# A two-layer encoder trunk: squares, latents and a table warm-up at the start, and another order of steps around the gated units of each half

## The chip, the cores and the metric

The kernel runs on one core of one Trainium2 chip. The metric is the device time of one execution in microseconds (us), as the median of several runs. A core has TensorE (PE; its weight loads are PEld), VectorE (DVE), ScalarE (ACT), GpSimd (POOL) and SyncE (SP), which here issues the loads of weights. All data is float32. A matrix product is made of three matmuls: every operand is split into a high half that the fast float32 format ("fp32r") holds, and a low half, the rest; high·high, high·low and low·high are added up in PSUM.

## The reference

One sequence of 512 tokens, 1024 channels, two layers. Layer 0 mixes with a short gated convolution and an 8-head latent attention side by side; layer 1 is a Conformer convolution module. Each has a squared-ReLU MLP of width 4096 behind it. Every part stands between two RMS norms.

```
def conformer_conv(h, w_pw1, b_pw1, w_dw, b_dw, ln_g, ln_b, w_pw2, b_pw2):
    u = h @ w_pw1 + b_pw1
    a, g = jnp.split(u, 2, axis=-1)
    u = a * jax.nn.sigmoid(g)                 # the gated units
    u = depthwise_conv(u, w_dw) + b_dw        # 31 taps over time
    u = jax.nn.silu(layer_norm(u, ln_g, ln_b))
    return u @ w_pw2 + b_pw2
...
for i in range(2):
    h = rms_norm(x, g[0])
    m = parallel_conv_mla(h, ...) if i == 0 else conformer_conv(h, ...)
    x = x + rms_norm(m, g[1])
    h = rms_norm(x, g[2])
    x = x + rms_norm(squared_relu_mlp(h, mlp_w1[i], mlp_w2[i]), g[3])
```

In layer 0, h goes through a combined projection: five blocks of 128 columns are the latents of queries (three) and of keys and values (two), each with an RMS norm of its own; a sixth is the rotary key; twelve more feed the gated convolution.

## The kernel before, in words

**Layout.** Everything is held transposed: 128 channels on the partitions, tokens along the free dimension, so x is eight tiles of 128 x 512. A weight *strip* (128 x 1024) makes one output tile: `strip` (L210) loads it (L222, SyncE's queue), ScalarE casts the high half (L223), GpSimd subtracts to get the low half (L224). A step of `linear` is 24 matmuls (L246 to L248): eight channel blocks times three. In PSUM there are three banks `S`, two `pj`, one `o` and two `mi` (`BANKS`). `scratch` (L174) hands out PSUM tiles in turn, from `o` and `mi`, and within a chain also from `pj`. `accum` (L165) hands out the banks for matmul sums, `S` and `pj` in turn, and `S` alone while convolutions or a chain are under way.

**The start.** `split_x` (L566) loads a tile of x, multiplies it by the norm's gain (L569) and splits it into halves (L230 on ScalarE, L233 on VectorE). Then, in a loop of its own, x is squared (`s0.square`, L357; added up in L332), the root is made from the sums (L367, L393 to L423), spread over the partitions by TensorE (L432) and copied to `R0` (L595). `latent` (L598) makes the five latent tiles with unscaled x, multiplies each by `R0` in place in PSUM (L603), squares it for its own norm and splits it (L230, L238).

**The middle phase.** From the first MLP on, the tokens are worked in two halves, A and B (256 tokens; 240 and 272 in layer 1, since the convolution reaches 15 tokens to both sides). The order is a list of steps, `M2`: `up` and `down` of an MLP quarter, `pw1` (gated units: two strips, a sigmoid L800, a product L804), `norm` (layer norm), `pw2`, and `join` (RMS norm, sum with x, next norm). `join`, `norm` and `finish` are chains: while their short operations wait for one another, `hold` and `pace` pull steps of the other half from the list, as long as the next one in it is of the other half and no chain itself. That is how TensorE gets work during a chain.

**The convolution** runs on VectorE, one tap an instruction (L822, L827), 31 taps for each of eight channel blocks and each half. Each `pw1` starts one convolution; every step adds credit (`FILL`, in us), and `fill` (L276) issues taps as long as the credit covers a tap's price (`TAP_US`), in turn from the two oldest convolutions. B's convolutions wait until A's layer norm has begun. When `norm` is reached with taps left over, it pulls steps of the other half and issues the rest between them. VectorE's instructions of this phase keep the order of the program; on the other engines, and everywhere in the start and in attention, the framework's scheduler orders the instructions.

**Tables.** ScalarE loads a table of functions when the next function isn't in the loaded one. `layer_norm` has a Silu on a tile of one column, `warm` (L847), ahead of its real ones (L862). `warm` is made and set to zero at L1034.

Of the kernel before, what the change touches and what calls it, by code (L numbers as in the profile page):

```python
# [12 lines left out]
AF = mybir.ActivationFunctionType  # L13
# [19 lines left out]
PAD = 16  # L33
M0 = [('wout', 'A'), ('join', 'A', 0, 1), ('wout', 'B')]
M1 = []
M2 = [('up', 'A', 0, 0, 0, 8), ('join', 'B', 0, 1), ('down', 'A', 0, 0, 0, 8), ('up', 'A', 0, 1, 0, 8), ('down', 'A', 0, 1, 0, 8), ('up', 'A', 0, 2, 0, 8), ('down', 'A', 0, 2, 0, 8), ('up', 'A', 0, 3, 0, 8), ('down', 'A', 0, 3, 0, 8), ('join', 'A', 0, 3), ('up', 'B', 0, 0, 0, 8), ('down', 'B', 0, 0, 0, 4), ('pw1', 'A', 0, 4), ('down', 'B', 0, 0, 4, 8), ('pw1', 'A', 4, 8), ('up', 'B', 0, 1, 0, 8), ('down', 'B', 0, 1, 0, 8), ('up', 'B', 0, 2, 0, 8), ('norm', 'A'), ('down', 'B', 0, 2, 0, 8), ('up', 'B', 0, 3, 0, 4), ('pw2', 'A', 0, 8), ('join', 'A', 1, 1), ('up', 'B', 0, 3, 4, 8), ('down', 'B', 0, 3, 0, 8), ('join', 'B', 0, 3), ('up', 'A', 1, 0, 0, 8), ('down', 'A', 1, 0, 0, 4), ('pw1', 'B', 0, 3), ('down', 'A', 1, 0, 4, 8), ('pw1', 'B', 3, 6), ('up', 'A', 1, 1, 0, 8), ('pw1', 'B', 6, 8), ('down', 'A', 1, 1, 0, 8), ('up', 'A', 1, 2, 0, 8), ('norm', 'B'), ('down', 'A', 1, 2, 0, 8), ('up', 'A', 1, 3, 0, 4), ('pw2', 'B', 0, 8), ('join', 'B', 1, 1), ('up', 'A', 1, 3, 4, 8), ('down', 'A', 1, 3, 0, 8), ('up', 'B', 1, 0, 0, 8), ('down', 'B', 1, 0, 0, 6), ('finish', 'A'), ('down', 'B', 1, 0, 6, 8), ('up', 'B', 1, 1, 0, 8), ('down', 'B', 1, 1, 0, 8), ('up', 'B', 1, 2, 0, 8), ('down', 'B', 1, 2, 0, 8)]
M3 = [('up', 'B', 1, 3, 0, 8), ('down', 'B', 1, 3, 0, 8), ('finish', 'B')]


OP_US, STEP_US = 0.39, 2.35  # L40
TAP_US = {T // 2 - PAD: 0.41, T // 2 + PAD: 0.44}
FILL = {'up': 2.3, 'down': 2.3, 'first': 2.6, 'sum': 1.8, 'pw1': 4.8, 'pw2': 2.3}
START = ['x', (128,), 'x', (256, 512, 768), 'x', 'x', 'x', 'x', 'x', 'x', ()]
ADD0 = 0
# [87 lines left out]
def trunk(ctx: ExitStack, tc: tile.TileContext, a, out: bass.AP):  # L132
    nc = tc.nc
# [59 lines left out]
    def small(w=NB):  # L193
        return new(sp, f"s{w}", 8 if w == 1 else 12, w)
# [32 lines left out]
    def split(dst, src, eng, scale=None, late=None):  # L227

        hi, lo = dst
        nc.scalar.activation(hi, src, AF.Copy, scale=1.0 if scale is None else scale)  # L230
        if late is not None:
            late.append(
                lambda: eng.tensor_tensor(out=lo, in0=src, in1=hi.bitcast(F32), op=ALU.subtract)  # L233
            )
        elif scale is None:
            eng.tensor_tensor(out=lo, in0=src, in1=hi.bitcast(F32), op=ALU.subtract)  # L236
        else:
            nc.vector.scalar_tensor_tensor(  # L238
                out=lo, in0=src, scalar=scale, in1=hi.bitcast(F32), op0=ALU.mult, op1=ALU.subtract
            )  # L240
# [31 lines left out]
    def settle(keep=0):  # L272
        while len(late) > keep:
            late.pop(0)()

    def fill(us):  # L276
        if scope.get("pulling"):
            return
        credit[0] += us
        while convs:  # L280
            turn[0] += 1
            conv, cost = convs[turn[0] % min(len(convs), 2)]
            if credit[0] < cost:
                break
            credit[0] -= cost
            if next(conv, None) is None:
                convs.remove((conv, cost))
        if not convs:
            credit[0] = min(credit[0], 0.0)

# [166 lines left out]
    def join(xs, ms, s, post, pre, hs, seg, h, mlp):  # L457

        hv = views(hs, seg)
        bc = rstds(s, lack.pop(h, None))

        t, ssq = {}, Sum(NC, seg, whole=WHOLE[0])
        for j in range(NC + 3):
            if j < NC:
                t[j] = scratch(seg.w)
                nc.vector.tensor_tensor(out=t[j], in0=ms[j][seg.sl], in1=bc, op=ALU.mult)
            i = j - 1  # L470
            if 0 <= i < NC:
                nc.vector.scalar_tensor_tensor(
                    out=t[i], in0=t[i], scalar=col(post + i), in1=xs[i][seg.sl], op0=ALU.mult, op1=ALU.add
                )
                nc.scalar.activation(xs[i][seg.sl], t[i], AF.Copy)
                if not mlp:
                    settle()
                    ssq.square(t[i], t[i])
            i = j - 2
            if mlp and 0 <= i < NC:  # L480
                nc.vector.scalar_tensor_tensor(
                    out=t[i], in0=t[i], scalar=col(pre + i), in1=R0[:, seg.sl], op0=ALU.mult, op1=ALU.mult
                )
                nc.scalar.activation(hv[i][0][seg.sl], t[i], AF.Copy)
            i = j - 3
            if mlp and 0 <= i < NC:
                nc.vector.tensor_tensor(
                    out=hv[i][1][seg.sl], in0=t[i], in1=hv[i][0][seg.sl].bitcast(F32), op=ALU.subtract
                )
            pace(4 if mlp else 3)  # L490
        if mlp:
            for j in range(NC):
                ssq.square(xs[j][seg.sl])
                settle(1)
                pace(1)
            hold()
            lack[h] = ratios(h, seg, ssq)
            return
        bc = rstds(ssq)
        for j in range(NC):  # L500
            t = scratch(seg.w)
            nc.vector.scalar_tensor_tensor(
                out=t, in0=xs[j][seg.sl], scalar=col(pre + j), in1=bc, op0=ALU.mult, op1=ALU.mult
            )
            settle()
            split((hv[j][0][seg.sl], hv[j][1][seg.sl]), t, nc.vector, late=late)
            pace(2)
        settle()
# [45 lines left out]
        ycat=("ycat", 4 * NB, T), sqf=("ycat", 4 * NB, T), acc1f=("ycat", 4 * NB, T),  # L554
        pt=("pt", 4, 2 * T), pr=("pr", 4, T + 2), tq=("tq", 1, T),
    )
    warm = small(1)
    nc.vector.memset(warm, 0.0)
    nc.scalar.activation(warm, warm, AF.Copy)
    nc.sync.dma_start(vec[:, :V_QN], a["vecs"][:, :V_QN])  # L560
    xs = [Win(xt()) for _ in range(NC)]
    hs = [hpair() for _ in range(NC)]
# [3 lines left out]
    def split_x(j):  # L566
        load_x(xs[j], j)
        t, (hi, lo) = scratch(T), (h.t[:, :T] for h in hs[j])
        nc.vector.tensor_scalar(out=t, in0=xs[j].t, scalar1=col(gains(0, 0) + j), scalar2=None, op0=ALU.mult)  # L569
        settle()  # L570
        split((hi, lo), t, nc.vector, late=late)

    win, j = [], 0
    for what in START:
# [23 lines left out]
    def latent(m0, n, gain, slot):  # L598
        lat, ss = [], Sum(n, FULL, whole=WL)
        for j in range(n):  # L600
            acc = linear(win[m0 + j] if m0 + j < len(win) else strip(a["win"][m0 + j]), hs)
            t = acc
            nc.vector.tensor_tensor(out=t, in0=acc, in1=R0, op=ALU.mult)  # L603
# [233 lines left out]
    def layer_norm(seg):  # L837

        hv = views(hs, seg)
        hold()  # L840
        mu = small()[:, : seg.nb]
        nc.vector.tensor_scalar(
            out=mu, in0=vsum[seg].done(), scalar1=-1.0 / D, scalar2=None, op0=ALU.mult
        )
        hold()
        total = spread(mu, seg)
        nc.scalar.activation(warm, warm, AF.Silu)  # L847
        s2 = Sum(NC, seg, whole=WHOLE[2])
        for c in range(NC):
            v = vs[c][:, seg.sl]  # L850
            nc.vector.tensor_tensor(out=v, in0=v, in1=total, op=ALU.add)
            settle()
            s2.square(v)
            pace(2)
        rb = rstds(s2)
        hold()
        for c in range(NC):
            v = vs[c][:, seg.sl]
            nc.vector.tensor_tensor(out=v, in0=v, in1=rb, op=ALU.mult)
            settle(1)  # L860
            t = scratch(seg.w)
            nc.scalar.activation(t, v, AF.Silu, bias=col(V_LNB + c), scale=col(V_LNG + c))  # L862
# [285 lines left out]
```

## Time and profile before

| what | us |
|---|---|
| median of 3 runs (1186.94 to 1188.17) | 1187.85 |
| the profiled execution | 1188.38 |
| its span, first to last instruction | 1186.6 |
| PE busy | 1142.9 |
| POOL busy | 845.4 |
| ACT busy | 664.6 |
| DVE busy | 648.3 |

A row of the table of stretches has the stretch, its length, the busy time of PE, PEld, DVE, ACT and POOL with the number of instructions in brackets, the granted TensorE clock as a share of the full one, the share of the DMA engines and GB/s. A row of the timeline has start, duration, engine, line, operation, out<-in and shapes, and in square brackets the engine's idle time ahead of it with what ended it. A row of the chain has start, duration, engine, tile and line. The matmul's end is modelled, so a PE that is "busy" all the time can still run slower; the number of matmuls in a stretch tells.

### The profile page before, as it was taken

The page shows a single profiled execution, that of the slowest core. Times are in us where ns is not written, and L with a number is a line of the kernel's source. Part 1 is how long each engine was busy: PE and PEld are TensorE (multiplying, and loading weights), DVE is VectorE, ACT ScalarE, POOL GpSimd, SP SyncE. Part 2 cuts the span into 40 slices and gives each one's busy share as a digit, 9 for nine tenths or more (in the row PEclk, how much of TensorE's full clock was granted, in tenths as well). Part 3 has the DMA queues.
Part 4 walks back from the last instruction along what each step waited for, and adds up shares of the span by engine and source line. Part 5 has one row for each costly group of instructions (what it writes and reads, how often), then busy time and mean ns, then how long its engine had stood idle before and what let it go on. Part 6 is the DMA issues. An engine that isn't in the chain of part 4 may idle for free.

```text
span 1186.6 us, 22844 instructions
## 1 busy us (share of the span) xinstructions
PE 1142.9 (96%) x8850; PEld 1102.7 (93%) x8850; DVE 648.3 (55%) x1699; ACT 664.6 (56%) x1217; POOL 845.4 (71%) x409
## 2 busy tenths in 40 slices
PE   7899989999999999899999999999997999999995
PEld 6688878999999999899999999999997999999995
DVE  5642699554522125499984275599995273222123
ACT  6421577556845457545466677546456685544352
POOL 5654554148988888698877778688886777878681
PEclk9899999999999999999999999999999999999998
DMA  6411332027655555465554555465555455553441
GB/s 210 160 59 36 94 116 72 1 91 243 205 178 194 181 178 194 126 208 183 185 190 160 178 177 179 149 195 194 195 186 168 143 172 177 187 183 134 137 148 38
DMA packets 55404, 183.99 MB, mean 155 GB/s; under 512 B 6400, under 2 KB 10880, under 8 KB 55296
## 3 DMA queue, kind: packets, MB, share of 16 engines
q1 hardware_dynamic: 54720, 181.86, 46.6%
q8 instruction: 69, 1.13, 0.4%
q10 hardware_dynamic: 576, 0.68, 0.2%
q14 instruction: 39, 0.32, 0.1%
HBM read 180.42 MB, written 2.10 MB: 154 GB/s over the span
## 4 chain that ended last, share of the span: by engine, by line
PE 86%; DVE 6%; ACT 4%; DMA 2%; POOL 1%; issue 1%; SPq 0%; POOLq 0%; ACTq 0%; DVEq 0%
PE S L246 22%; PE S L247 21%; PE S L248 21%; PE pj L246 6%; PE pj L247 6%; PE pj L248 6%; ACT whi L223 2%; DVE pr L762 1%; DMA raw<-in_win 1%; POOL wlo L224 1%; DVE s L756 1%; PE mi L432 1%; PE mi L367 1%; DVE pt L236 1%; PE mi L765 1%
## 5 line engine op out<-in xcount | busy, mean ns | idle before, releaser
L224 POOL TENSOR_TENSOR wlo<-raw,whi 128x1024 fp32r<-128x1024 f32 (+2 forms) x347 | 802.4, 2325 | 268.7 <-ACT whi L223 260.8
L223 ACT ACTIVATE whi<-raw 128x1024 fp32r<-128x1024 f32 (+2 forms) x347 | 355.9, 1030 | 391.1 <-PE S L247 200.0
L246 PE MATMUL S<-h,whi 128*128 128x256 f32 (+3 forms) x1208 | 348.2, 291 | 11.8 <-DVE u L804 4.6
L247 PE MATMUL S<-h,whi 128*128 128x256 f32 (+3 forms) x1208 | 349.1, 290 | 0.1
L248 PE MATMUL S<-h,wlo 128*128 128x256 f32 (+3 forms) x1208 | 349.1, 290 | 0.0
L246 PEld LDWEIGHTS S<-h,whi 128*128 128x128 f32 x1208 | 228.4, 191 | 18.3 <-ACT h L230 5.2
L246 PE MATMUL S<-hid,whi 128*128 128x256 f32 (+2 forms) x840 | 234.8, 282 | 2.3 <-DVE acc L332 2.1
L247 PE MATMUL S<-hid,whi 128*128 128x256 f32 (+2 forms) x840 | 235.5, 281 | 0.0
L248 PE MATMUL S<-hid,wlo 128*128 128x256 f32 (+2 forms) x840 | 234.8, 280 | 0.0
L247 PEld LDWEIGHTS S<-h,whi 128*128 128x128 f32 x1208 | 229.7, 190 | 3.8 <-DVE h L233 0.5
L248 PEld LDWEIGHTS S<-h,wlo 128*128 128x128 f32 x1208 | 229.6, 190 | 3.7 <-POOL wlo L224 0.2
L827 DVE SCALAR_TENSOR_TENSOR pj<-u,taps,pj 128x240 f32<-128x240 f32 (+1 forms) x464 | 195.3, 485 | 2.0
L246 PEld LDWEIGHTS S<-hid,whi 128*128 128x128 f32 x840 | 157.8, 189 | 3.7 <-DVE acc L332 2.9
L248 PEld LDWEIGHTS S<-hid,wlo 128*128 128x128 f32 x840 | 158.6, 189 | 0.0
L247 PEld LDWEIGHTS S<-hid,whi 128*128 128x128 f32 x840 | 158.5, 189 | 0.1
L246 PE MATMUL pj<-h,whi 128*128 128x272 f32 (+3 forms) x344 | 107.7, 313 | 10.1 <-ACT h L230 5.5
L247 PE MATMUL pj<-h,whi 128*128 128x272 f32 (+3 forms) x344 | 107.6, 313 | 0.0
L248 PE MATMUL pj<-h,wlo 128*128 128x272 f32 (+3 forms) x344 | 106.5, 309 | 0.0
L246 PEld LDWEIGHTS pj<-h,whi 128*128 128x128 f32 x344 | 66.4, 193 | 13.7 <-ACT h L230 5.8
L247 PEld LDWEIGHTS pj<-h,whi 128*128 128x128 f32 x344 | 66.5, 193 | 3.9 <-DVE h L233 0.9
L248 PEld LDWEIGHTS pj<-h,wlo 128*128 128x128 f32 x344 | 66.5, 193 | 3.3 <-issue 0.2
L236 DVE TENSOR_TENSOR hid<-S,hid 128x256 fp32r<-128x256 f32 (+2 forms) x102 | 42.8, 421 | 47.8 <-ACT hid L230 47.2
(250 smaller groups left out, 1629.6 us busy)
## 6 DMA issues: line engine op xcount, KB each, us to landing
raw<-in_w SPq DMA_DIRECT2D x256, 512.0 KB, 3.3
raw<-in_pw SPq DMA_DIRECT2D x48, 512.0 KB, 3.3
raw<-in_win SPq DMA_DIRECT2D x16, 512.0 KB, 3.3
x<-in_xT SPq DMA_DIRECT2D x16, 256.0 KB, 4.4
raw<-in_wout SPq DMA_DIRECT2D x8, 512.0 KB, 3.3
raw<-in_wq SPq DMA_DIRECT2D x8, 192.0 KB, 2.4
out<-x SPq DMA_DIRECT2D x8, 120.0 KB, 2.5
out<-x SPq DMA_DIRECT2D x5, 136.0 KB, 1.7
```

The lines of the kernel that those rows point to most:

```text
L223: nc.scalar.activation(h, r, AF.Copy)
L224: nc.gpsimd.tensor_tensor(out=lo[:, c0:c1], in0=r, in1=h.bitcast(F32), op=ALU.subtract)
L236: eng.tensor_tensor(out=lo, in0=src, in1=hi.bitcast(F32), op=ALU.subtract)
L246: nc.tensor.matmul(acc, sh, mh, start=i == 0, stop=False)
L247: nc.tensor.matmul(acc, sh, ml, start=False, stop=False)
L248: nc.tensor.matmul(acc, sl, mh, start=False, stop=i == n - 1)
L367: nc.tensor.matmul(s[:, b : b + 1], q[:, sl.start - self.seg.lo : sl.stop - self.seg.lo], one, start=i == 0, stop=i == len(self.parts) - 1,)
L432: nc.tensor.matmul(o[:, sl], r[:, b : b + 1].to_broadcast([bw, P]), ident[:bw, :bw], start=True, stop=True,)
L756: nc.vector.reduce_max(out=mx, in_=S, axis=AX.X)
L762: eng.tensor_scalar(out=pr_, in0=pr_, scalar1=sm, scalar2=None, op0=ALU.mult)
L765: nc.tensor.transpose(tp[:, kb * P : (kb + 1) * P], pr_[:, kb * P : (kb + 1) * P], ident)
L827: nc.vector.scalar_tensor_tensor(out=dst, in0=src, scalar=wk, in1=acc, op0=ALU.mult, op1=ALU.add)
```

## The change

Five edits. Layer 0's start: (1) x is squared in `split_x`, right after its split, and the loop behind it is gone. (2) A latent's product goes to an SBUF tile (`ycat`) instead of back into its PSUM bank. Middle phase: (3) a Sigmoid on `warm` stands in `join` ahead of the gated units' norm. (4) A tap has two prices, one while two convolutions take turns and one while only one is left. (5) The list `M2`: the eight `pw1` of a half stand in one piece and come after two `down` steps instead of four (they were in two pieces in A, three in B, with steps between them); `norm` A stands after two instead of eight `up` steps of the third quarter, `norm` B after six instead of eight, with the `pw1` of B sooner; `pw2` A stands ahead of all `up` steps of the fourth quarter.

```
-M2 = [... ('up','B',0,0,0,8), ('down','B',0,0,0,4), ('pw1','A',0,4), ('down','B',0,0,4,8), ('pw1','A',4,8),
-  ('up','B',0,1,0,8), ('down','B',0,1,0,8), ('up','B',0,2,0,8), ('norm','A'), ('down','B',0,2,0,8),
-  ('up','B',0,3,0,4), ('pw2','A',0,8), ('join','A',1,1), ('up','B',0,3,4,8), ('down','B',0,3,0,8), ('join','B',0,3),
-  ('up','A',1,0,0,8), ('down','A',1,0,0,4), ('pw1','B',0,3), ('down','A',1,0,4,8), ('pw1','B',3,6),
-  ('up','A',1,1,0,8), ('pw1','B',6,8), ('down','A',1,1,0,8), ('up','A',1,2,0,8), ('norm','B'), ('down','A',1,2,0,8),
-  ('up','A',1,3,0,4), ('pw2','B',0,8), ...]
+M2 = [... ('up','B',0,0,0,8), ('down','B',0,0,0,2), ('pw1','A',0,8), ('down','B',0,0,2,8),
+  ('up','B',0,1,0,8), ('down','B',0,1,0,8), ('up','B',0,2,0,2), ('norm','A'), ('up','B',0,2,2,8), ('down','B',0,2,0,8),
+  ('pw2','A',0,8), ('join','A',1,1), ('up','B',0,3,0,8), ('down','B',0,3,0,8), ('join','B',0,3),
+  ('up','A',1,0,0,8), ('down','A',1,0,0,2), ('pw1','B',0,8), ('down','A',1,0,2,8),
+  ('up','A',1,1,0,8), ('down','A',1,1,0,8), ('up','A',1,2,0,6), ('norm','B'), ('up','A',1,2,6,8), ('down','A',1,2,0,8),
+  ('up','A',1,3,0,4), ('pw2','B',0,8), ...]
-TAP_US = {T // 2 - PAD: 0.41, T // 2 + PAD: 0.44}
+TAP_US = {T // 2 - PAD: (0.385, 0.51), T // 2 + PAD: (0.41, 0.54)}
 ... fill:
-            conv, cost = convs[turn[0] % min(len(convs), 2)]
+            conv, costs = convs[turn[0] % min(len(convs), 2)]
+            cost = costs[len(convs) == 1]
 ... join, where the gated units' norm follows:
         bc = rstds(ssq)
+        nc.scalar.activation(warm[0], warm[0], AF.Sigmoid)
 ... split_x:
         split((hi, lo), t, nc.vector, late=late)
+        s0.square(xs[j].t)
 ... behind the loop over START:
-    for j in range(NC):
-        s0.square(xs[j].t)
-        settle()
 ... latent:
-            t = acc
+            t = tmp("ycat")
             nc.vector.tensor_tensor(out=t, in0=acc, in1=R0, op=ALU.mult)
```

(The elements of `M2` are: what, half, layer, quarter, first step, end; for `pw1` and `pw2`: what, half, first, end.) The old one-column tile of the start is called `first` now, and `warm` is a list that holds the same tile as before.

More of the change, by code (lines that the diff above doesn't have):

```diff
@@ L35 @@
 M1 = []
-M2 = [('up', 'A', 0, 0, 0, 8), ('join', 'B', 0, 1), ('down', 'A', 0, 0, 0, 8), ('up', 'A', 0, 1, 0, 8), ('down', 'A', 0, 1, 0, 8), ('up', 'A', 0, 2, 0, 8), ('down', 'A', 0, 2, 0, 8), ('up', 'A', 0, 3, 0, 8), ('down', 'A', 0, 3, 0, 8), ('join', 'A', 0, 3), ('up', 'B', 0, 0, 0, 8), ('down', 'B', 0, 0, 0, 4), ('pw1', 'A', 0, 4), ('down', 'B', 0, 0, 4, 8), ('pw1', 'A', 4, 8), ('up', 'B', 0, 1, 0, 8), ('down', 'B', 0, 1, 0, 8), ('up', 'B', 0, 2, 0, 8), ('norm', 'A'), ('down', 'B', 0, 2, 0, 8), ('up', 'B', 0, 3, 0, 4), ('pw2', 'A', 0, 8), ('join', 'A', 1, 1), ('up', 'B', 0, 3, 4, 8), ('down', 'B', 0, 3, 0, 8), ('join', 'B', 0, 3), ('up', 'A', 1, 0, 0, 8), ('down', 'A', 1, 0, 0, 4), ('pw1', 'B', 0, 3), ('down', 'A', 1, 0, 4, 8), ('pw1', 'B', 3, 6), ('up', 'A', 1, 1, 0, 8), ('pw1', 'B', 6, 8), ('down', 'A', 1, 1, 0, 8), ('up', 'A', 1, 2, 0, 8), ('norm', 'B'), ('down', 'A', 1, 2, 0, 8), ('up', 'A', 1, 3, 0, 4), ('pw2', 'B', 0, 8), ('join', 'B', 1, 1), ('up', 'A', 1, 3, 4, 8), ('down', 'A', 1, 3, 0, 8), ('up', 'B', 1, 0, 0, 8), ('down', 'B', 1, 0, 0, 6), ('finish', 'A'), ('down', 'B', 1, 0, 6, 8), ('up', 'B', 1, 1, 0, 8), ('down', 'B', 1, 1, 0, 8), ('up', 'B', 1, 2, 0, 8), ('down', 'B', 1, 2, 0, 8)]
@@ new lines @@
+M2 = [('up', 'A', 0, 0, 0, 8), ('join', 'B', 0, 1), ('down', 'A', 0, 0, 0, 8), ('up', 'A', 0, 1, 0, 8), ('down', 'A', 0, 1, 0, 8), ('up', 'A', 0, 2, 0, 8), ('down', 'A', 0, 2, 0, 8), ('up', 'A', 0, 3, 0, 8), ('down', 'A', 0, 3, 0, 8), ('join', 'A', 0, 3), ('up', 'B', 0, 0, 0, 8), ('down', 'B', 0, 0, 0, 2), ('pw1', 'A', 0, 8), ('down', 'B', 0, 0, 2, 8), ('up', 'B', 0, 1, 0, 8), ('down', 'B', 0, 1, 0, 8), ('up', 'B', 0, 2, 0, 2), ('norm', 'A'), ('up', 'B', 0, 2, 2, 8), ('down', 'B', 0, 2, 0, 8), ('pw2', 'A', 0, 8), ('join', 'A', 1, 1), ('up', 'B', 0, 3, 0, 8), ('down', 'B', 0, 3, 0, 8), ('join', 'B', 0, 3), ('up', 'A', 1, 0, 0, 8), ('down', 'A', 1, 0, 0, 2), ('pw1', 'B', 0, 8), ('down', 'A', 1, 0, 2, 8), ('up', 'A', 1, 1, 0, 8), ('down', 'A', 1, 1, 0, 8), ('up', 'A', 1, 2, 0, 6), ('norm', 'B'), ('up', 'A', 1, 2, 6, 8), ('down', 'A', 1, 2, 0, 8), ('up', 'A', 1, 3, 0, 4), ('pw2', 'B', 0, 8), ('join', 'B', 1, 1), ('up', 'A', 1, 3, 4, 8), ('down', 'A', 1, 3, 0, 8), ('up', 'B', 1, 0, 0, 8), ('down', 'B', 1, 0, 0, 6), ('finish', 'A'), ('down', 'B', 1, 0, 6, 8), ('up', 'B', 1, 1, 0, 8), ('down', 'B', 1, 1, 0, 8), ('up', 'B', 1, 2, 0, 8), ('down', 'B', 1, 2, 0, 8)]
@@ L286, in fill @@
             if next(conv, None) is None:
-                convs.remove((conv, cost))
+                convs.remove((conv, costs))
         if not convs:
@@ L556, in trunk @@
     )
-    warm = small(1)
-    nc.vector.memset(warm, 0.0)
-    nc.scalar.activation(warm, warm, AF.Copy)
+    first = small(1)
+    nc.vector.memset(first, 0.0)
+    nc.scalar.activation(first, first, AF.Copy)
     nc.sync.dma_start(vec[:, :V_QN], a["vecs"][:, :V_QN])
@@ L846, in layer_norm @@
         total = spread(mu, seg)
-        nc.scalar.activation(warm, warm, AF.Silu)
+        nc.scalar.activation(warm[0], warm[0], AF.Silu)
         s2 = Sum(NC, seg, whole=WHOLE[2])
@@ L877, in start @@
                 convolve(*todo.pop(0))
-    hid, sums, kept, us, lack = {}, {}, {}, [], {}
+    hid, sums, kept, us, lack, warm = {}, {}, {}, [], {}, []
     def seg_of(h, layer):
@@ L1032, in trunk @@
     us.extend(tmp("u") for _ in range(NC))
-    warm = new(sp, "warm", 1, 1)
-    nc.vector.memset(warm, 0.0)
+    warm.append(new(sp, "warm", 1, 1))
+    nc.vector.memset(warm[0], 0.0)
     vs = [m.t for m in ms]
```

## The prediction

> **What bounds the kernel now.** I read the page first, then a table of stretches, then the chain of waits, then the timelines of the places that the table pointed to.
>
> ```profile
> PE 1142.9 (96%) x8850; PEld 1102.7 (93%) x8850; DVE 648.3 (55%) x1699; ACT 664.6 (56%) x1217; POOL 845.4 (71%) x409
> core 0: us, PE busy (x) PEld busy (x) DVE busy (x) ACT busy (x) POOL busy (x), PEclk, DMA share, GB/s
> 80.00:100.00 20.00, 20.00 (x89) 16.30 (x88) 6.09 (x6) 2.64 (x4) 10.17 (x9) 1.00 0.17 54
> 480.00:520.00 40.00, 36.43 (x303) 35.79 (x302) 25.73 (x69) 20.78 (x32) 30.45 (x13) 1.00 0.50 164
> 520.00:540.00 20.00, 20.00 (x171) 20.00 (x171) 18.45 (x49) 9.36 (x14) 16.94 (x8) 1.00 0.56 184
> 640.00:660.00 20.00, 18.43 (x135) 17.30 (x134) 9.29 (x33) 14.68 (x30) 10.92 (x6) 0.91 0.42 135
> 760.00:780.00 20.00, 17.79 (x142) 17.59 (x142) 16.77 (x39) 11.29 (x16) 18.97 (x9) 0.91 0.56 185
> 840.00:860.00 20.00, 20.00 (x181) 20.00 (x180) 19.91 (x51) 9.56 (x13) 17.96 (x9) 1.00 0.58 193
> 900.00:940.00 40.00, 33.81 (x257) 33.24 (x256) 17.21 (x53) 29.21 (x60) 22.55 (x10) 0.91 0.36 121
> 1020.00:1040.00 20.00, 20.00 (x164) 20.00 (x163) 9.11 (x34) 10.22 (x18) 15.80 (x7) 1.00 0.68 210
> ```
>
> TensorE is the bound, and no matmul is added or removed; only its idle time and its half clock can move. The full stretches give the matmul's price: 20/89 = 0.225 us for 512 columns, 20/171 = 0.117 for 256, 20/181 = 0.110 for 240, 20/164 = 0.122 for 272. A step (24 matmuls) is 2.81 us at 256 columns, 2.65 at 240. Counts times price against length give what is lost: 40 − 303·0.117 = 4.6 (first gated units, A), 20 − 135·0.117 = 4.2 (layer norm A), 3.9 (gated units B, widths mixed), 9.6 (layer norm B, about 67 at 240, 178 at 272, 12 small). That is 22.3 us in the middle phase. The other loss that the change touches is at the start:
>
> ```profile
> 15.70 2.43 POOL wlo L224
> 43.97 0.75 DVE x L238
> 49.82 0.43 PE pj L248
> ...
> 39.15 1.05 PE L432 MATMUL mi<-kst,s 128*128 128x128 f32 x8
> 44.76 0.79 PE L246 MATMUL pj<-h,whi 128*128 128x512 f32 x1 [4.55 <-DVE x L238]
> 50.85 0.39 PE L248 MATMUL pj<-h,wlo 128*128 128x512 f32 x1
> ...
> 40.87 0.70 DVE L603 TENSOR_TENSOR pj<-pj,R 128x512 f32<-128x512 f32 x1 [6.19 <-ACT R L595]
> 25.17 0.69 DVE L332 TENSOR_TENSOR ycat<-ycat,mi 128x512 f32<-128x512 f32 x1
> 34.53 0.15 DVE L423 TENSOR_TENSOR inv<-mi,s 128x7 f32<-128x7 f32 x1
> ```
>
> All five latent sums stand in PSUM and wait for R0. The squares are added up at 25.9, the root is ready at 34.7, but its spread (L432) stands in TensorE's queue behind all 120 latent matmuls, at 39.15. Then product, square, high and low half must pass before a bank is free: 4.55 us idle, then 14 matmuls in 6.1 us at half clock instead of 3.2. Lost: 7.4.
>
> **The start, part by part.** *Latents to SBUF.* The bank is free after the first product, not after L238: 40.87 + 0.70 = 41.6 instead of 44.7, up to 3.1 us. The 0.70 is priced the same for SBUF, where no row shows it. *Squares earlier.* They alternate with the products in the bank order: now products take `mi` and `o` in turn; afterwards squares and products draw alternately, so x1 to x7's products all get `o`, which has one bank. Each then passes multiply, high half and low half alone: 2.4 us in the rows below, 16.87 to 19.27. *Table.* The join ahead of the gated units gains a Sigmoid on a [128,1] tile. What such a warm-up does is visible now:
>
> ```profile
> 2.25 1.28 ACT L847 ACT_TABLE_LOAD   x1
> 3.54 0.44 ACT L847 ACTIVATE warm<-warm 128x1 f32<-128x1 f32 x2
> 3.95 0.63 ACT L357 ACTIVATE ycat<-x 128x512 f32<-128x512 f32 x1
> 16.87 0.76 DVE L569 TENSOR_SCALAR o<-x,vec 128x512 f32<-128x512 f32 x1
> 18.58 0.69 DVE L233 TENSOR_TENSOR h<-o,h 128x512 fp32r<-128x512 f32 x1 [0.36 <-ACT h L230]
> ...
> L800 ACT ACT_TABLE_LOAD  x2: 1283/1283/1283, 499.6 to 761.0; - x2
> L862 ACT ACT_TABLE_LOAD  x2: 1283/1283/1283, 644.8 to 912.4; - x2
> ```
>
> Both Silu warm-ups of the layer norms run at 3.5 us: they depend on nothing, so the scheduler hoisted them, and L862 still loads its table twice. I take the same for the Sigmoids. In program order they alternate, and L800 and L862 show that each switch loads: 4·(1.28 + 0.20) = 5.9 us from 2.25, so ScalarE begins at 8.2 instead of 3.95, 4.2 later, and L800 keeps its loads. The table edit gains nothing and costs up to 4.2.
>
> With that, x0's halves are done near 10.4 (square, cast and two halves behind 8.2), then seven times 2.4: the last at 27.2 (now 19.3), the sum of squares near 28.5 (now 25.9). TensorE works meanwhile on strips 0 and 1, and from 18.1 + 4.2 = 22.3 on the third: 36 + 21 matmuls by 27.2, 63·0.225 = 14.2 more, so the latents end at 41.4 (now 39.1). The squares now come earlier in the queue's order, so I expect L432 ahead of the last latents; R0 and the freed bank then come before 41.4, no idle time, no half clock: 44.8 + 2.9 − 41.4 = 6.3 gained. If L432 stays last, TensorE resumes near 44: 0.8 plus perhaps the clock. Ends: −7 (4.2 and 3 both on the path, R0 no sooner) and +7.4. I take 4.5, between the two orders of L432 and nearer to the first. What follows is full of matmuls (the row of 80 to 100), so a shift carries on.
>
> The Trainium skill (ScalarE: Activation LUTs, "What ACT_TABLE_LOAD costs") prices a table load at about 2.7 us. The rows say 1.283; by the page's figure the start would gain 3·1.4 = 4.2 less and the sum would be 1179.7.
>
> **The middle phase.** `pw1` in one piece, `norm` moved, two tap prices. I walked the lists through the planner's own rules (credit per step over price per tap; one step of the other half pulled where the chain waits). Per half, now to after: steps behind the second root of join 0 3 and ahead of `pw1`: 4 to 2 (A and B). Other-half steps from the first `pw1` to the end of the taps: A 29 to 27, B 33 to 29. Steps inside the layer norm and behind it before `pw2`: A 9+2 to 9+2, B 7+0 to 9+4. Taps run with one convolution alone: A 25 to 11, B 35 to 8. VectorE's order is fixed by the program here, so these hold.
>
> *First gated units.*
>
> ```profile
> 481.37 0.16 DVE L418 SCALAR_TENSOR_TENSOR s<-mi,s 128x2 f32<-128x2 f32 x1
> 483.36 0.60 PE L432 MATMUL mi<-kst,s 128*128 128x128 f32 x4
> 485.15 0.63 PE L246 MATMUL S<-h,whi 128*128 128x256 f32 x3 [1.18 <-ACT h L230]
> 501.36 0.48 DVE L804 SCALAR_TENSOR_TENSOR u<-S,vec,y 128x256 f32<-128x256 f32 x1 [10.00 <-ACT y L800]
> 763.38 0.38 PE L246 MATMUL S<-h,whi 128*128 128x256 f32 x1 [2.21 <-DVE u L804]
> ```
>
> Now a `down` takes the `pj` bank that the first gate needs, the gate comes late, and TensorE waits 2.2 for u. After, no `down` stands between: the gate follows at once, and the next two sums fill 5.6 us while table, sigmoid and u take 2.6, so this wait goes. But two steps less (5.6 us) cover the join: TensorE would run dry near 480.5, the spread can come at 481.6, h again 1.8 later: 2.5 idle instead of 1.2. A gap of 2.2 at 763.38 brought a half-clock stretch (clock 0.91 there: 9% of 20 us, 1.8 lost), the like in A did not, so I add half of it, 0.9. A 4.6 becomes 2.5 + 0.9 + 0.5 that stays, B by the same reckoning 3.9 becomes 2.9. Gain 1.7; ends −3 and +6. The 16 strips in a row ask for one per 2.81 us; SyncE's loads wait for GpSimd's 2.43 a strip, so both queues keep up, at nothing.
>
> The Trainium skill (TensorE: Matmul & The Clock Gate, "Why this matters for your kernels") wants no idle gap above about 3 us, so a 2.5 us gap would keep the clock. The trace agrees for the 4.55 us gap and not for the one at 763.38: 2.21 us idle, and the clock of its stretch is 0.91. By the rule the sum would be 1.8 lower; I go by the row.
>
> *Layer norms.*
>
> ```profile
> 627.56 0.16 DVE L842 TENSOR_SCALAR s<-mi 128x2 f32<-128x2 f32 x1 [3.96 <-PE mi L367]
> 655.51 0.41 DVE L233 TENSOR_TENSOR h<-mi,h 128x240 fp32r<-128x240 f32 x1 [0.39 <-ACT h L230]
> 896.54 0.16 DVE L842 TENSOR_SCALAR s<-mi 128x3 f32<-128x3 f32 x1 [4.71 <-PE mi L367]
> 921.50 0.44 DVE L233 TENSOR_TENSOR h<-o,h 128x272 fp32r<-128x272 f32 x1 [0.46 <-ACT h L230]
> 502.50 5.05 DVE L827 SCALAR_TENSOR_TENSOR pj<-u,taps,pj 128x240 f32<-128x240 f32 x10
> 544.17 4.21 DVE L827 SCALAR_TENSOR_TENSOR pj<-u,taps,pj 128x240 f32<-128x240 f32 x11
> 763.96 4.84 DVE L827 SCALAR_TENSOR_TENSOR pj<-u,taps,pj 128x272 f32<-128x272 f32 x9
> 789.05 4.58 DVE L827 SCALAR_TENSOR_TENSOR pj<-u,taps,pj 128x272 f32<-128x272 f32 x11
> 890.23 0.40 DVE L532 TENSOR_TENSOR m<-S,m 128x240 f32<-128x240 f32 x1
> ```
>
> The norm's chain is 28.4 us in A, 25.4 in B. B's 7 steps hide 18.6 and 9.6 is lost; 13 steps are 34. Against it: the taps. With two convolutions a tap is 4.58/11 = 0.416 (alone 0.538), so B needs 240·0.416 + 8·0.538 + 45 others at up to 0.40 = 122 us on VectorE from some 8 us after `pw1` begins, 130 at most; TensorE is through its 16·2.81 + 29·2.65 = 122 then. VectorE ends 6 to 8 late, TensorE has eaten some 2.5 of the 13 steps, 28 us are left for a chain of some 28, and the last steps wait for banks: 4 lost. Gain 5.6; ends 0 and 9.6. A: 237·0.383 + 11·0.505 + 43·0.40 + 8 = 122 against 121, even; its 11 steps stay, but the two inside the last part are `down`, not `up`, three ScalarE instructions less each, where Silu and cast queue on ScalarE: I take half of the 4.2, gain 2 (ends 0 and 4.2). VectorE full in both stretches holds TensorE up here and there: −1. Join A 1 1 has 16 steps behind it instead of 12: nothing, it is covered now.
>
> **Sum.** 4.5 + 1.7 + 5.6 + 2 − 1 = 12.8. The profiled execution took 1188.4 (span 1186.6 and 1.8 around it), the median is 1187.85, 0.5 less: 1188.4 − 12.8 − 0.5 = 1175.1; I say 1175.5.
>
> **Rivals.** (1) Forecast, 1171 to 1180: 0.54. (2) The norms stay as long as they are, since banks, not steps, limit TensorE there: only 4.5 + 1.7 remain less the 1, 1182.5: 0.17. For it: in A 11 steps are there and 4.2 is lost. (3) The start costs 3 instead of gaining 4.5, ScalarE late by 4.2 with all of it on the path: 1183: 0.08. (4) All gaps close, start 7, middle 15: 1166: 0.07. (5) Gaps only move; the change doesn't do what it says: 1188: 0.07. (6) Slower: VectorE becomes the bound. Each 0.01 us more per tap is 2.4 us per half; at 0.45 and 0.48 instead of 0.383 and 0.416 it ends 16 later in each half ; 32 late, some 7 of it under cover, against the 12.8: 1188 + 25 − 12.8 = 1200. It decides from about 0.03 per tap on. For it: VectorE is 19.91 of 20 busy at 840. Against: at 520 it is 18.45, with 1.5 to spare. 0.07.
>
> **Numbers.** A measurement here tells about 0.2% (2.4 us) from no change. Faster: (1) to (4), 0.86; same (5), 0.07; slower (6), 0.07. The range 1167 to 1185 leaves out most of (4), (5) and (6).
>
> **What would show it.** At the start: four table loads before the first square, L432 ahead of the last latent matmul, no idle row at the first `pj` sum behind it. First u some 5 us nearer to the join, TensorE's wait for u gone, a wait of 2 to 3 for h in its place. 900 to 940 with some 310 matmuls in place of 257. Wrong, if waits of TensorE for VectorE fill the tap stretches, if the warm Sigmoid runs in the join, or if attention, which the diff leaves alone but whose order on four engines the scheduler draws anew, loses more than it does now.

## The result: 1176.1 us, and the profile after

| | before | after |
|---|---|---|
| median, us (four runs each) | 1187.91 (1186.94 to 1188.17) | 1176.1 (1173.68 to 1176.42) |
| span of the profiled execution | 1186.6 | 1174.4 |
| mean granted clock | 0.986 | 0.991 |

The ratio is 0.9898, with a 95% interval of 0.988 to 0.9915: the changed kernel is 11.8 us faster, and the prediction of 1175.5 was 0.6 us off. Its terms were less exact than their sum: their errors nearly cancel, and that is luck.

The stretches that the prediction read, found again by their work (each lies 5 to 25 us earlier). First after, then before, with the same lengths:

```profile
core 0: us, PE busy (x) PEld busy (x) DVE busy (x) ACT busy (x) POOL busy (x), PEclk, DMA share, GB/s
475.00:515.00 40.00, 37.17 (x298) 36.53 (x297) 29.22 (x82) 20.18 (x29) 28.50 (x12) 0.96 0.47 159
622.00:642.00 20.00, 18.24 (x153) 17.85 (x152) 10.94 (x38) 13.55 (x25) 15.38 (x7) 1.00 0.56 184
733.00:758.00 25.00, 22.53 (x177) 21.98 (x176) 13.18 (x39) 13.61 (x23) 13.69 (x6) 0.93 0.35 118
880.00:920.00 40.00, 38.29 (x327) 37.91 (x327) 18.39 (x57) 28.49 (x52) 32.50 (x15) 1.00 0.55 183
```

```profile
758.00:783.00 25.00, 22.79 (x185) 22.59 (x185) 19.73 (x46) 13.78 (x18) 21.68 (x10) 0.93 0.51 169
890.00:930.00 40.00, 33.81 (x267) 33.24 (x266) 18.06 (x56) 24.82 (x50) 22.17 (x11) 0.91 0.38 125
```

The number of matmuls in a stretch tells what it gave. Gated units of half A: 303 to 298, 5 matmuls at 0.117, 0.6 us lost. Half B: 185 to 177, 0.9 lost. Norm A: 135 to 153, some 2.1 gained. Norm B: 267 to 327, 60 matmuls at some 0.116, 7.0 gained. Together 7.6.

The start is read by a landmark that both kernels have: the spread of the first root in attention, the same four small matmuls behind the same wait of TensorE for `pt`. Before, then after:

```profile
158.61 0.63 PE L765 MATMUL mi<-kst,pr 128*128 128x128 f32 x4 [1.77 <-DVE pt L236]
```

```profile
155.18 0.63 PE L766 MATMUL mi<-kst,pr 128*128 128x128 f32 x4 [1.77 <-DVE pt L237]
```

So the start gave 3.4 us. The span is 12.2 shorter: 3.4 + 7.6, and 1.2 in small pieces that I did not follow.

ScalarE's start after (timeline), with the table loads, and then TensorE's and VectorE's rows of the same stage:

```profile
2.25 1.28 ACT L502 ACT_TABLE_LOAD   x1
3.76 1.28 ACT L848 ACT_TABLE_LOAD   x1
5.28 1.28 ACT L502 ACT_TABLE_LOAD   x1
6.79 1.28 ACT L848 ACT_TABLE_LOAD   x1
8.20 0.61 ACT L359 ACTIVATE ycat<-x 128x512 f32<-128x512 f32 x1
...
20.11 1.72 PE L369 MATMUL mi<-kst,ycat 128*128 128x1 f32 x14
32.14 1.05 PE L434 MATMUL mi<-kst,s 128*128 128x128 f32 x8
44.33 0.95 PE L369 MATMUL mi<-kst,ycat 128*128 128x1 f32 x8
45.14 0.48 PE L247 MATMUL pj<-h,whi 128*128 128x512 f32 x1
...
19.38 0.68 DVE L334 TENSOR_TENSOR ycat<-ycat,mi 128x512 f32<-128x512 f32 x1
28.02 0.69 DVE L234 TENSOR_TENSOR h<-o,h 128x512 fp32r<-128x512 f32 x1 [0.67 <-ACT h L231]
```

All four warm-ups run at the very start, and ScalarE squares x0 at 8.20, as forecast. The sum of squares is ready at 20.1. The spread of R0 (L434) runs before the last latents, and the first `pj` sum behind them starts with no idle time in its row, at the full clock.

### The profile page after: what moved, and what is told of

It reads as the page before. It is cut to its first block, busy times and chain, and to the rows that moved or that the text cites. A ratio compares the mean times of both kernels' runs of the same rounds, so it can differ in the third digit from the quotient of the medians.

```text
span 1174.4 us, 22870 instructions
## 1 busy us (share of the span) xinstructions
PE 1135.2 (97%) x8850; PEld 1096.5 (93%) x8850; DVE 648.6 (55%) x1701; ACT 667.8 (57%) x1220; POOL 846.6 (72%) x409
## 4 chain that ended last, share of the span: by engine, by line
PE 86%; ACT 4%; DVE 4%; POOL 2%; DMA 2%; issue 1%; POOLq 0%; ACTq 0%; DVEq 0%
PE S L247 22%; PE S L248 21%; PE S L249 21%; PE pj L247 6%; PE pj L248 6%; PE pj L249 6%; POOL wlo L225 2%; DMA raw<-in_w 1%; ACT whi L224 1%; DVE pr L763 1%; PE mi L369 1%; PE mi L434 1%; PE mi L766 1%; PE o L248 1%; DVE s L757 1%
## 5 line engine op out<-in xcount | busy, mean ns | idle before, releaser
L247 PE MATMUL S<-hid,whi 128*128 128x256 f32 (+2 forms) x824 | 230.3, 282 | 2.3 <-DVE acc L334 1.8
L248 PE MATMUL S<-hid,whi 128*128 128x256 f32 (+2 forms) x824 | 230.9, 281 | 0.0
L249 PE MATMUL S<-hid,wlo 128*128 128x256 f32 (+2 forms) x824 | 230.4, 281 | 0.0
L828 DVE SCALAR_TENSOR_TENSOR pj<-u,taps,pj 128x240 f32<-128x240 f32 (+1 forms) x464 | 190.9, 483 | 1.0
L247 PEld LDWEIGHTS S<-hid,whi 128*128 128x128 f32 x824 | 154.8, 189 | 3.3 <-DVE acc L334 2.2
L249 PEld LDWEIGHTS S<-hid,wlo 128*128 128x128 f32 x824 | 155.6, 189 | 0.0
L248 PEld LDWEIGHTS S<-hid,whi 128*128 128x128 f32 x824 | 155.5, 189 | 0.1
L247 PE MATMUL pj<-h,whi 128*128 128x272 f32 (+3 forms) x344 | 105.8, 308 | 11.9 <-ACT h L231 10.2
L248 PE MATMUL pj<-h,whi 128*128 128x272 f32 (+3 forms) x344 | 105.1, 306 | 0.5 <-DVE h L234 0.5
L247 PEld LDWEIGHTS pj<-h,whi 128*128 128x128 f32 x344 | 64.9, 189 | 15.7 <-ACT h L231 11.0
L248 PEld LDWEIGHTS pj<-h,whi 128*128 128x128 f32 x344 | 65.0, 189 | 4.2 <-DVE h L234 1.8
```

What stands on the lines that cost most here:

```text
L247: nc.tensor.matmul(acc, sh, mh, start=i == 0, stop=False)
L248: nc.tensor.matmul(acc, sh, ml, start=False, stop=False)
L249: nc.tensor.matmul(acc, sl, mh, start=False, stop=i == n - 1)
L828: nc.vector.scalar_tensor_tensor(out=dst, in0=src, scalar=wk, in1=acc, op0=ALU.mult, op1=ALU.add)
```

## The experiments

All were run with five rounds beside the kernel before. Each of the three groups had its own runs of it: medians 1186.7, 1188.05 and 1187.43. These differ by 1.4 us, so across groups the ratios compare.

| kernel | median, us | ratio | 95% interval |
|---|---|---|---|
| start only | 1181.93 | 0.9955 | 0.9938 to 0.9971 |
| middle only | 1178.61 | 0.9931 | 0.9912 to 0.9949 |
| no Sigmoid | 1171.3 | 0.9869 | 0.9851 to 0.9887 |
| table in place | 1169.17 | 0.9854 | 0.9835 to 0.9872 |
| four downs | 1170.12 | 0.9848 | 0.983 to 0.9866 |
| norm B, less cover | 1177.02 | 0.9913 | 0.9897 to 0.993 |
| old prices | 1178.51 | 0.9921 | 0.9905 to 0.9936 |
| three downs, more cover | 1171.15 | 0.9862 | 0.9843 to 0.988 |
| squares only | 1181.6 | 0.9949 | 0.9935 to 0.9962 |
| four downs in B | 1168.98 | 0.9844 | 0.983 to 0.9857 |
| two banks | 1173.34 | 0.988 | 0.9867 to 0.9894 |

**Start only.** The kernel before with edits (1) and (2): squares in `split_x`, latents to `ycat`; no Sigmoid, old list, old prices.

> The kernel before with the squares right behind each split and the latents to SBUF; no Sigmoid, old prices, old list. Theory (the Sigmoid warm-ups hold ScalarE 3 us longer at the start, all of it on TensorE's path to the latents): here that cost is absent, so the start gains 6 to 7, near 1181. Rival (ScalarE's late start is hidden behind the loads of x and the strips): the gain is the 3.5 that the traces of before and after show at the start, near 1184.5.

4.8 us faster by the medians, 5.3 by the ratio. The landmark stands at 153.27, 5.3 earlier. Without the extra table loads the start is worth more than in the changed kernel, though by less than I had thought.

**Middle only.** The kernel before with the new list and the two prices.

> The kernel before with the new list and the two tap prices; squares, latents and warm-ups as before. If the parts add up, the middle gains 12.2 - 3.5 = 8.7: near 1179.2. Rival (part of the middle's gain hangs on the order that the start hands on, or on the Sigmoid): 1182 or more. The norm-B stretch should again show some 320 matmuls in 40 us.

8.1 us faster, near the expected 8.7, and 40 us at norm B (884 to 924) hold 327 matmuls again. The two parts add up to 12.9. The kernel to hold against that sum is the next one, "no Sigmoid", which is both parts and nothing else: it gains 15.4 in the same group of runs. The 2.5 us between are no more than these intervals leave open (some 2 us on either side of each ratio), so the parts add up roughly; that neither leans on the other is not shown.

Norm A in this kernel has the same steps as in the changed one, and nearly the same wait (1.65 us), but here the half clock falls on it:

```profile
625.00:645.00 20.00, 18.29 (x140) 17.90 (x139) 9.24 (x34) 12.26 (x23) 14.00 (x6) 0.91 0.56 184
```

**No Sigmoid.**

```
         bc = rstds(ssq)
-        nc.scalar.activation(warm[0], warm[0], AF.Sigmoid)
```

> The changed kernel without the Sigmoid line. Theory: two table loads and two Sigmoids and one of the two Silu loads leave the start, ScalarE's first square moves from 8.2 to about 4 us, the latents end 3 to 4 earlier: 1172 to 1173. Rival (hidden): 1176. No Sigmoid load moves in the middle, since L801 loads its table either way.

By the medians 4.8 us faster than the changed kernel, by the ratios 3.4, whose intervals overlap a little. With the landmark below this shows that the warm Sigmoid costs time, and it gives nothing. ScalarE of this kernel has one hoisted load instead of four and starts on x0 at 4.13:

```profile
2.24 1.28 ACT L847 ACT_TABLE_LOAD   x1
3.54 0.44 ACT L847 ACTIVATE warm<-warm 128x1 f32<-128x1 f32 x2
4.13 0.63 ACT L359 ACTIVATE ycat<-x 128x512 f32<-128x512 f32 x1 [0.15 <-DMA x<-in_xT]
...
152.38 0.63 PE L765 MATMUL mi<-kst,pr 128*128 128x128 f32 x4 [1.74 <-DVE pt L237]
```

The landmark comes 2.8 us before that of the changed kernel: of 4.1 us that ScalarE gets free, 2.8 reach TensorE. The rest goes with the granted clock (below): executions of the two kernels with the same mean clock differ by 2.4 to 3.2 us (1175.99 to 1176.42 against 1173.33 at 0.991; 1173.68 against 1170.47 and 1171.3 at 0.994). Whether the edit itself changes the clock is not shown.

**Table in place.** Both warm-ups read data of their place, so that the scheduler can't take them to the start.

```
+        settle()
+        nc.scalar.activation(warm[0], ssq.parts[0][:, :1], AF.Sigmoid)
         bc = rstds(ssq)
-        nc.scalar.activation(warm[0], warm[0], AF.Sigmoid)
...
-        nc.scalar.activation(warm[0], warm[0], AF.Silu)
+        nc.scalar.activation(warm[0], mu[:, :1], AF.Silu)
```

> The changed kernel, but both warm-ups read data of their place (Sigmoid the sum of squares of the join, Silu the mean of the layer norm), so that they can't be hoisted. Theory: the start as without the Sigmoid (3 to 4), and the loads leave the real sigmoid and Silu: the waits of 1.1 and 0.6 for u go, and up to 1.3 in each norm: 1169 to 1171. Rival (the loads in the middle are hidden anyway, or fall on ScalarE where the chain needs it): like the kernel without the Sigmoid, 1172 to 1176.

1169.17, the median 6.9 us below that of the changed kernel. The load now lies in the join, ahead of the root, and the real sigmoids and Silus load nothing (groups of ScalarE, table loads alone):

```profile
L502 ACT ACT_TABLE_LOAD x2 | 2.6, 1283 | 0.0
L849 ACT ACT_TABLE_LOAD x2 | 2.6, 1283 | 0.0
L563 ACT ACT_TABLE_LOAD x1 | 1.3, 1283 | 0.7 <-PEq L1138 0.7
L635 ACT ACT_TABLE_LOAD x1 | 1.3, 1283 | 0.0
L761 ACT ACT_TABLE_LOAD x1 | 1.3, 1283 | 0.0
```

TensorE no longer waits for u. Against "no Sigmoid" this is 0.0015 in the ratio, inside both intervals: that the start must be free of the loads is shown, that placing them well gains more is not.

**Four downs.** "Table in place" with four instead of two `down` steps ahead of `pw1`, in both halves: `('down', 'B', 0, 0, 0, 4), ('pw1', 'A', 0, 8), ('down', 'B', 0, 0, 4, 8)`, and B likewise.

> As table-in-place (1169.2), but four instead of two down-projection steps of the other half stand ahead of the gated units in both halves (the join of layer 0 then finds the eleven steps it asks for, instead of ten, and one is left over). Theory (the steps between a join and the norm are one budget: what covers the join is missing behind the norm): the idle of 2.5 us at each first gated unit shrinks to 0 to 1.4 and no half clock is granted there, a gain of 2 to 5 us; but each convolution starts two steps later, the norm hands out three to four of its fourteen steps before its last tap, and the norms lose 3 to 10 us in all: time 1169 to 1176. Rival (cover behind the norm has slack): the norms stay as they are, time 1164 to 1167.

1170.12, no difference from "table in place". TensorE's idle time ahead of the first gated unit of B is gone. But norm A now has the row below, where "table in place" waits 1.43 us, with the half clock right behind it, and a wait of 0.78 us for u stands at the first gated unit of each half:

```profile
634.85 0.49 PE L247 MATMUL S<-h,whi 128*128 128x240 f32 x2 [1.85 <-ACT h L231]
```

The theory names the direction in half A: what covers the join is missing behind the norm. But that is 0.42 us, far less than the 3 to 10 that it expected of the norms, and behind norm B one wait of 0.34 is left in place of 0.92. From 470 to 1000 us TensorE's idle rows of 0.25 us and more add up to some 6.7 us instead of 8.5, and yet the time does not fall. Why not stays open.

**Norm B, less cover.** The changed kernel with six `down` steps instead of eight `down` and four `up` between norm B and `pw2`:

```
- ('down', 'A', 1, 2, 0, 8), ('up', 'A', 1, 3, 0, 4), ('pw2', 'B', 0, 8), ('join', 'B', 1, 1), ('up', 'A', 1, 3, 4, 8)
+ ('down', 'A', 1, 2, 0, 6), ('pw2', 'B', 0, 8), ('join', 'B', 1, 1), ('down', 'A', 1, 2, 6, 8), ('up', 'A', 1, 3, 0, 8)
```

> The changed kernel (1176.1), but the pointwise projection of half B stands after the sixth down step instead of after eight and four up steps, so that only eight steps of half A, not fourteen, stand between norm B and its consumers. Theory (norm B's gain of 7 us came from the steps behind it): PE waits 5 to 10 us again behind norm B and drops to the half clock there, time 1182 to 1187. Rival (the gain came from the taps ending sooner, through the prices and the gated units in one piece): loss under 2 us, time 1175 to 1178.

By its time the rival holds: 1177.02, and neither interval parts it from the changed kernel. By the profile the mechanism of the theory holds. These are TensorE's idle rows at norm B in this kernel with their stretch, then in the kernel before, then in the changed one:

```profile
885.94 0.91 PE L434 MATMUL mi<-kst,s 128*128 128x128 f32 x6 [2.43 <-DVE s L420]
888.80 1.05 PE L247 MATMUL S<-h,whi 128*128 128x272 f32 x3 [1.96 <-ACT h L231]
...
880.00:900.00 20.00, 15.61 (x111) 15.37 (x110) 9.95 (x34) 12.37 (x24) 8.00 (x4) 0.83 0.32 106
```

```profile
913.30 0.91 PE L432 MATMUL mi<-kst,s 128*128 128x128 f32 x6 [2.43 <-DVE s L418]
916.16 1.05 PE L246 MATMUL S<-h,whi 128*128 128x272 f32 x3 [1.96 <-ACT h L230]
```

```profile
900.55 0.38 PE L247 MATMUL pj<-h,whi 128*128 128x240 f32 x1 [1.46 <-DVE h L234]
```

With the steps taken away, the waits of before come back to the hundredth, 2.43 and 1.96, and the half clock with them: the steps behind norm B are what removed them. Why the time hardly shows it: the steps that are not spent there stand behind join B 1 1, where the stretch from 940 to 960 holds 176 matmuls instead of 160 (1.8 us), and this execution drew the half clock nowhere else in the middle, where that of the changed kernel drew it twice. I had counted neither. The spreads (L434) show the balance. At norm B's first spread this execution is 4.0 us ahead of the changed kernel's (872.75 against 876.79), and at the spread of `finish` A, behind join B 1 1, it is 0.6 ahead (1016.98 against 1017.59). So the missing steps cost some 3.4 us, less than the 5 to 10 that I expected. The draw also differs between executions: the two with a mean clock of 0.988 took 1179.4 and 1179.5, the four others 1175.1 to 1177.3.

**Old prices.** The changed kernel with 0.41 and 0.44 for every tap.

> The changed kernel (1176.1), but each convolution tap keeps its former price (0.41 and 0.44 us, alone or in pairs). Theory (a price above what a tap takes in pairs, 0.383 and 0.416 us, hands taps out too late, so that the norm pulls two steps more ahead of its last tap in half A and four more in half B): the norms lose 3 to 8 us, time 1179 to 1184. Rival (VectorE works at its own pace and the price only orders the issue): within 2 us, 1174 to 1178. A third way, faster: the high price keeps room on VectorE for the other half's steps, under 1173.

1178.51, 2.4 us above the changed kernel by the medians, 2.7 by the ratios, whose intervals overlap: between theory and rival. TensorE waits for h at two places in norm A, 0.44 and 0.95 us, and at two in norm B, 0.98 and 0.34; in the changed kernel it is one each, 1.70 and 1.46. These waits are no longer in sum (1.39 and 1.32), so they do not explain the loss; at B's first gated unit TensorE waits 0.76 for `y` and 0.46 for u instead of 0.40. By the medians and ratios some 2.5 of the middle's 8.8 us come from the prices, and the list makes the rest; where in the profile the prices act was not followed further.

**Three downs, more cover.** "Table in place" with three `down` steps ahead of `pw1`, and `pw2` five (A) and one (B) `up` steps later.

> As table-in-place (1169.2), but three instead of two down steps ahead of the gated units in both halves, and the second pointwise projections stand five up steps further back in half A and one in half B, so that each join finds its eleven steps and the norms keep 15 and 12 steps (11 and 13 before). Theory: the idle at the first gated units falls by 1 us a half, and without it no half clock is granted there; norm A's 2 us go; norm B's 1.2 may grow by one step's length: time 1163 to 1168. Rival (one step does not suffice, the first gated unit waits for h whatever the list says): 1167 to 1170.

A miss: 1171.15. Norm A's wait falls to 0.66 us, but a new one of 0.95 for a sum of squares stands at 690.77, and at B's first gated unit one of 1.92 for the sigmoid's `y`, with the half clock behind it; at join B one of 2.24 stands in place of 1.27 and 0.54, with the half clock there too. I did not follow why that sigmoid comes late.

**Squares only.** The kernel before with edit (1) alone.

> The kernel before (1187.9), with one part of the change alone: each square of x is taken inside the splitting loop instead of behind it. The latents stay in their accumulator banks; list, prices and the Sigmoid line are as before. Theory (the 4.55 us idle and the half clock behind the latents came from R0, which waited for the squares; with the squares early R0 is there before the last latent): most of the start's 5 to 6 us, time 1181.5 to 1183.5. Rival (the latents' banks are what PE waits for, and only the move to the ycat tiles frees them): within 1.5 us of before, 1186.5 to 1188.5.

1181.6, as much as both edits of the start together. In this kernel L432 runs at 29.46 and TensorE has no idle row from there to the last latent. Its landmark, at 152.56, is even 0.7 us ahead of that of "start only". Writing the latents to SBUF adds nothing here: once R0 is there in time, their banks are free in time.

**Four downs in B.** "Table in place" with four `down` steps in half B alone.

> As table-in-place (1169.2), with four instead of two down steps ahead of the gated units in half B alone (in half A four cost at norm A what they gave at the join; behind norm B the loss stayed at 1.7 us with four). Theory: the 2.8 us at B's first gated unit go, and 0 to 1 us comes back as a wait for u: time 1166 to 1168.5. Rival (the steps are one budget in B too, as in half A): 1168.5 to 1170.5.

1168.98: by its time the rival. The profile shows both: no idle row of TensorE ahead of B's first gated unit, then 0.78 us for u, and at norm B waits of 0.25, 0.95 and 0.31 in place of 0.33 and 0.92. The medians differ by 0.2 us. It is the lowest time measured here, and not told apart from "table in place".

**Two banks.** "Table in place" with `s0.square(xs[j].t, tmp("ycat"))`: squares in SBUF, so the products of `split_x` have both scratch banks.

> As table-in-place (1169.2), but the squares of x go to tiles in SBUF, so that the products x1 to x7 of the splitting loop change between two scratch banks instead of sharing one. By the prediction's step (the chain on the one bank sets the last half of x, and that sets the end of the latents) the last half comes 3 to 5 us sooner and the latents end 2 to 4 us sooner: time 1165 to 1167.5. Rival (PE has no idle time behind its first 15 us, so the latents end when PE has done their matmuls): the last half comes sooner and the time stays, 1168.5 to 1170.

Neither: 4.2 us slower by the medians, 3.1 by the ratios. The sum of the squares now reads two SBUF tiles, and three of its seven adds take 6.4 us together instead of 2.1 (VectorE of this kernel, then its GpSimd):

```profile
8.47 1.97 DVE L334 TENSOR_TENSOR ycat<-ycat,ycat 128x512 f32<-128x512 f32 x1
12.27 0.69 DVE L334 TENSOR_TENSOR ycat<-ycat,ycat 128x512 f32<-128x512 f32 x1
17.85 4.45 DVE L334 TENSOR_TENSOR ycat<-ycat,ycat 128x512 f32<-128x512 f32 x2
...
7.80 5.75 POOL L225 TENSOR_TENSOR wlo<-raw,whi 128x896 fp32r<-128x896 f32 x5 [2.41 <-ACT whi L224]
16.40 5.34 POOL L225 TENSOR_TENSOR wlo<-raw,whi 128x1024 fp32r<-128x1024 f32 x2 [2.85 <-ACT whi L224]
```

The last low half of x starts at 25.43 instead of 25.68, and R0 comes 5 us later. To give the products two banks this way costs more than it frees, so the run does not tell what the chain on the one bank costs. That the chain exists is seen in the changed kernel: all seven products go to `o`, and most start within 0.05 us of the end of the low half before them (the last low half but one ends at 26.22, and the last product starts at 26.26).

## Why the prediction was right, point by point

**The table.** Forecast: the Sigmoids are hoisted, four loads, ScalarE at 8.2, L800 keeps its loads. All four came true (ScalarE at 8.20), and "no Sigmoid" shows the price, 2.8 us at the landmark. The four loads follow each other every 1.51 us with their Sigmoid or Silu (2.25, 3.76, 5.28, 6.79), so the higher price of 2.7 a load is out here.

**The start, 4.5 forecast, 3.4 measured.** The gain's mechanism was right: R0 in time, no 4.55 us gap, no half clock. Two steps were off. The squares do not wait for the splits: the sum was forecast for 28.5 and is done at 20.1. And the latents end at 44.3 instead of 41.4. I had let the last half of x (27.2 forecast; it ends at 28.7) set that end, with 57 of the 120 latent matmuls done by 27.2; 50 were. But TensorE has no idle time from 19.6 to 44.3 in the changed kernel, so what counts is when it began, 9.5 instead of 5.5, and its matmuls. The last half of x did not hold it up. The step on the latents' banks, "up to 3.1 us", was not needed: "squares only" gets everything without it.

**First gated units, +1.7 forecast, −1.5 measured (0.6 and 0.9 lost).** The step was mis-sized at two places. The wait for u was to vanish; it went from 2.21 to 0.92 in A and from 2.21 to 0.40 for `y` in B, since the real sigmoid still loads its table (1.28 us) ahead of it. And the half clock, counted at half its price, came in both halves. That is a draw: "no Sigmoid" has the same waits there, 0.91 and 1.00 us in A and 1.07 and 1.00 in B, and the half clock in neither half. From that spread to the next it takes 135.45 us in A where the changed kernel takes 136.96, and 136.75 in B where that takes 138.05, so the two draws cost 1.5 and 1.3 us. The wait ahead of the first unit came near the forecast 2.5: 0.91 for the root and 1.00 for h. The first u came 2.7 us nearer to the join's spread in A (15.3 us behind it instead of 18.0), not 5. The sum itself had a slip: the reckoning for A, 2.5 + 0.9 + 0.5, gives 3.9 for B too, which is what B lost before, and not 2.9; without it the forecast gain was 0.7.

**Norm B, 5.6 forecast, 7.0 measured; norm A, 2 forecast, 2.1 measured.** The mechanism is shown for norm B by "norm B, less cover". Its half clock was hardly a draw: all three profiled kernels with the old list have it there, "norm B, less cover" too, and none of the nine others. I had let VectorE end 6 to 8 us late and charged 4 us for it; one idle row of 1.46 us is what was left. For norm A the size agrees, but the reason given, that `down` steps spare ScalarE, is shown by no run. The waits are no shorter than before (1.70 us against 0.58 and 0.75); what fell away is the half clock, 0.91 before and 1.00 after. "Middle only" has the same list, draws the half clock there, and holds 140 matmuls where the changed kernel holds 153 and the kernel before 135: 0.6 us gained instead of 2.1. All three profiled kernels with the old list draw it at norm A, and two of the ten with the new one ("middle only", "four downs"). So the change seems to make it rarer; how is not shown.

**VectorE full, −1 forecast.** Not seen. The stretch after the gated units of A holds the same 171 matmuls per 20 us as before. Rival (6), in which VectorE becomes the bound, is out with it.

**The sum.** The terms missed by 1.1 (start), 3.2 (gated units), and on the other side by 1.4 (norm B), 0.1 (norm A) and 1 (VectorE); with the 1.2 us of small pieces the span is 12.2 us shorter instead of 12.8. The mechanisms of the start and of norm B carry the gain; that the sum came so close is luck.

**Rivals (2) and (5)** fall with norm B's rows and with the time, (3) with the landmark, (4) with the gated units.

## What to carry to other kernels

A warm-up that depends on nothing is not where it stands in the source: give it an operand that exists only at its place, or the scheduler collects it at the start, where it costs. Steps that cover waits are one budget along the list, as the steps moved from norm B to join B show; when some are moved to one wait, look for the next wait that they covered, and count that as part of the price. And before a chain is shortened, look whether the engine that it feeds is idle at all.

## What the hardware showed that I had not expected

**The same gap, with and without the half clock.** The changed kernel and "no Sigmoid" have the same waits to the hundredth at A's first gated unit. Timeline rows of TensorE and the stretches there, in the changed kernel:

```profile
478.13 0.71 PE L434 MATMUL mi<-kst,s 128*128 128x128 f32 x4 [0.91 <-DVE s L420]
479.84 0.62 PE L247 MATMUL S<-h,whi 128*128 128x256 f32 x3 [1.00 <-ACT h L231]
...
478.00:482.00 4.00, 2.87 (x16) 2.64 (x17) 3.01 (x9) 2.69 (x6) 4.00 (x2) 0.85 0.23 47
482.00:486.00 4.00, 4.00 (x28) 4.00 (x27) 3.33 (x9) 1.54 (x4) 0.43 (x1) 0.73 0.58 219
```

In "no Sigmoid", 4 us earlier:

```profile
474.11 0.71 PE L434 MATMUL mi<-kst,s 128*128 128x128 f32 x4 [0.91 <-DVE s L420]
475.82 0.61 PE L247 MATMUL S<-h,whi 128*128 128x256 f32 x3 [1.00 <-ACT h L231]
...
474.00:478.00 4.00, 2.90 (x21) 2.66 (x22) 3.02 (x9) 2.66 (x6) 4.00 (x2) 1.00 0.20 47
478.00:482.00 4.00, 4.00 (x36) 4.00 (x35) 3.29 (x9) 1.54 (x4) 0.41 (x1) 1.00 0.56 219
```

28 matmuls in 4 us against 36, and 16 against 21 ahead of them, with the same waits: some 1.5 us. The clock lost in the two rows, 0.15 and 0.27 of 4 us, is 1.7 us, or 3.4 us at half clock. The Trainium skill (TensorE: Matmul & The Clock Gate, "What's actually happening") says that the clock follows the activity in windows of 3413 ns that run free of the kernel's start. The length agrees with that. It would also explain why the same gap costs in one execution and not in the other, by where in a window it falls; no run here shows the windows themselves. The mean clocks of one kernel's executions differ likewise (0.991 to 0.994 in the changed kernel, 1176.42 to 1173.68 us). So differences of 1 to 3 us between two kernels here can be drawn lots, and the profile must be asked how often the half clock came before an edit gets the credit.

**VectorE and GpSimd.** An add of 128x512 with one operand in PSUM takes 0.68 to 0.69 us in the changed kernel, also while GpSimd subtracts a strip. In "two banks" both operands lie in SBUF. Three of its seven adds run while GpSimd is idle and take 0.68 us. Three start while GpSimd subtracts: they take 1.97, 1.64 and 2.78 us, and each ends 0.55 us after that subtraction does (9.89, 18.94 and 21.75). The add at 12.27 starts just as one subtraction ends and takes 0.69; the next subtraction, of 256 columns, then takes 1.18 us instead of 0.73. The Trainium skill (SBUF — State Buffer, "SBUF: two separate sides") says that an operation of VectorE with two SBUF inputs and one of GpSimd that reads SBUF lock each other out. These rows agree. The prediction's price of 0.70 us for a product into SBUF (measured 0.68 to 0.69) was not put to that, since its other operand lies in PSUM.
